# A long convolution shared by two engines: GpSimd's products move to ScalarE, through a ring of six places

## The chip, the cores and the metric

The kernel runs on one core of a Trainium2 chip. The metric is the device time of one execution in microseconds. Five engines work side by side, each through its own queue of instructions in order: TensorE (PE, with its weight loads as PEld), VectorE (DVE), ScalarE (ACT), GpSimd (POOL) and SyncE (SP), which issues most transfers. An instruction waits for others by semaphores; what stands behind it in the queue waits with it.

## The reference

Two blocks follow each other on 512 rows of width 1024. Only the first holds the change: a gated long convolution beside a linear recurrence. The second (attention, then a mixture of 32 experts) takes the larger part of the time and is the same in both kernels.

```python
def first_block(x, c, ...):
    shift, scale, gate = split(silu(c) @ mod_w + mod_b, 3)
    h = rmsnorm(x, norm_g) * (1 + scale) + shift
    cv, cg, cs, lx, ls = split(h @ w_in)          # five times 1024 columns
    v = cv * sigmoid(cg)
    v = causal_depthwise_conv(v, dw_w, dw_b)      # 31 taps per channel
    v = silu(layernorm(v, cln_g, cln_b))
    y_conv = (v @ pw2_w + pw2_b) * silu(cs)
    xs = causal_depthwise_conv(lx, sc_w, sc_b)    # 4 taps
    r = sigmoid(xs @ wr + br); i = sigmoid(xs @ wi + bi)      # per head
    log_a = -8 * r * softplus(-lam)
    hs = linear_scan(exp(log_a), sqrt(-expm1(2 * log_a)) * i * xs)
    y = concatenate([y_conv, hs * silu(ls)]) @ w_out
    return rmsnorm(x + (1 + gate) * y, final_g)   # into second_block
```

A tap of the long convolution multiplies a shifted row of v by one number per channel and adds it to a sum.

## The kernel before

Channels lie on the 128 partitions, the 512 rows along the free dimension; 1024 channels are eight blocks c = 0 to 7. Matrix products are made in three passes from weights and activations split in two parts: `W` (a list of weight loads) casts a piece of 128x2048 to its high part on ScalarE (`whi`, L126) and makes the low part on VectorE (`wlo`, L127).

Eight **conv steps** come first. Step c multiplies h by two pieces of 128 columns (48 matmuls into the PSUM tiles `pcv` and `pcg`), casts the next weights, takes the sigmoid of `pcg` on ScalarE (`sg`, L570) and multiplies on VectorE into `v` (L574). Then `conv31(c)` sets up the 31 taps of that block. The last tap, with the bias, is a scaled activation on ScalarE (`start`, L528). The other 30 are shared out:

- blocks 0, 2 and 4, and two taps of block 7, on GpSimd (`pool_tap`): a product into one scratch place (L537), then a sum into `acc` (L539). These instructions are written into GpSimd's queue at once.
- blocks 1, 3, 5, 6 and the rest of 7 on VectorE: one instruction a tap (`tap`, L532), with the sum in PSUM. They stand in a list, `bg`; `drain(n)` takes n entries from it at fixed places of the code (`DR_0` = 3, `DR_V` = 8, `DR_LX` = 2, `DR_G` = 1, `DR_S` = 6). `join` adds what GpSimd made of block 7 (L543).

Four **recurrence steps** follow, each with two blocks: `lru_in` (product `plx`, its copy L594, the short convolution of three multiply-adds on VectorE L598, the split into two parts L197 and L198), a `silu_proj` of the convolution's outer gate, and `lru_gates` (two small products, two sigmoids L621 and L622). Then `silu_proj(ylru_, 0)` takes what is left in `bg`. GpSimd also keeps a running sum `csum` of some finished blocks (`add_up`, L517 and L519); `means` (L690) needs it and all of `acc`. After that come variances, normalisation and the rest.

The code is written in the order in which the engines run it; no scheduler moves it. `ylru` (eight places) is written by `silu_proj(ylru_, i)` only from the end of the recurrence steps on.

Of the kernel before, what the change touches and what calls it, by code (L numbers as in the profile page):

```python
# [9 lines left out]
F32 = mybir.dt.float32  # L10
# [3 lines left out]
AF = mybir.ActivationFunctionType  # L14
OP = mybir.AluOpType
# [4 lines left out]
S = 512  # L20
# [5 lines left out]
LN_EPS = 1e-5  # L26
ALPHA = 2.0 ** 0.25
LRU_C = 8.0
POOL_CONV = (0, 2, 4)
POOL_TAPS = {7: 2}  # L30
PY = 8
POOL_LN = (0, 1)
BIG = 1024.0
# [121 lines left out]
def block_kernel(ctx, tc, A, out, dbg=None, upto=99):  # L155
    nc = tc.nc
    pe, dve, act, pool, sp = nc.tensor, nc.vector, nc.scalar, nc.gpsimd, nc.sync
    dbg = dbg or {}

    def dump(name, ap):  # L160
        if name in dbg:
            sp.dma_start(out=dbg[name], in_=ap)
# [8 lines left out]
    def psa(name="pa", shape=(128, 512)):  # L171
        return ps.tile(list(shape), F32, tag="a", name=name, bufs=4)

    def pss(name="pss"):
        return ps.tile([128, 2, 512], F32, tag="s", name=name, bufs=2)
# [7 lines left out]
    def mm3(o, l, r, first, last):  # L183

        (lh, ll), (rh, rl) = l, r
        pe.matmul(o, lh, rh, start=first, stop=False)
        pe.matmul(o, lh, rl, start=False, stop=False)
        pe.matmul(o, ll, rh, start=False, stop=last)
# [23 lines left out]
    def k8(t, n=256):  # L212
        return t[:, :8 * n].rearrange("p (k n) -> p k n", k=8)
# [106 lines left out]
    for k in range(8):  # L320
        t = px.tile([128, 2048], F32, tag="mraw", name="mraw", bufs=6)
        for c in range(0, 2048, 2048 if k < 7 else 512):
            n = 2048 if k < 7 else 512
# [39 lines left out]
    def columns(i):  # L363
        pt = psa("ptr")
        pe.transpose(pt[:, 0:128], R3 if i == 3 else R[:, i, :], ident)
        act.copy(out=C[:, i, :], in_=pt[:, 0:128])
# [16 lines left out]
    def dw_col(j, c):  # L383
        n = 8 * j + c
        return C[:, 1 + n // 128, n % 128:n % 128 + 1]
# [31 lines left out]
    for hf in range(2):  # L417
# [4 lines left out]
        for a in range(2):  # L422
            dst = (sB, sA)[hf][:, 4 * a:4 * a + 4]
            dve.tensor_reduce(out=dst, in_=pm[:, a, :].rearrange("p (m n) -> p m n", m=4), axis=mybir.AxisListType.X,
                              op=OP.add)
# [46 lines left out]
    bg = []  # L472

    def drain(n):

        turn = 0
        while n and bg:
            ch_ = bg[turn % min(2, len(bg))]
            ch_.pop(0)()
            if not ch_:  # L480
                bg.remove(ch_)
            turn, n = turn + 1, n - 1

    def proj(o, w, m, xs, nk, n):
        (wh, wl) = w
        wv = [t[:, :nk * n].rearrange("p (k n) -> p k n", k=nk) for t in (wh, wl)]
        for k in range(nk):
            mm3(o, [t[:, k, 128 * m:128 * m + 128] for t in wv], [t[:, k, :] for t in xs], k == 0, k == nk - 1)

    acc = pY.tile([128, 8, NK], F32, tag="acc", name="acc")[:, :, 0:S]  # L490
    scs = [pA.tile([128, 4, S], F32, tag=t, name=t) for t in ("scsh", "scsl")]
    r8 = pA.tile([128, 8, S], F32, tag="r8", name="r8")
    ylru = pY.tile([128, 8, NK], F32, tag="ylru", name="ylru")[:, :, 0:S]

    spare = [pA.tile([128, 4 * S], F32R, tag=t, name=t) for t in ("spareh", "sparel")]
# [9 lines left out]
    def vv(name):  # L505
        return pA.tile([128, S + 32], F32, tag="vv", name=name, bufs=VV)
# [6 lines left out]
    def add_up(c):  # L513

        summed.append(c)
        if len(summed) == 2:
            pool.tensor_tensor(out=csum, in0=acc[:, summed[0], :], in1=acc[:, c, :], op=OP.add)  # L517
        elif len(summed) > 2:
            pool.tensor_tensor(out=csum, in0=csum, in1=acc[:, c, :], op=OP.add)  # L519

    def conv31(c):

        v, st_ = vt[c], {}
        np_ = 30 if c in POOL_CONV else POOL_TAPS.get(c, 0)

        def start():
            st_["o"] = acc[:, c, :] if np_ == 30 else pss("pc")[:, 0, :]
            act.activation(out=st_["o"], in_=v[:, 30:30 + S], func=AF.Identity, scale=dw_col(30, c),  # L528
                           bias=dw_b[:, c:c + 1])

        def tap(j):
            dve.scalar_tensor_tensor(out=acc[:, c, :] if j == 29 and not np_ else st_["o"], in0=v[:, j:j + S],  # L532
                                     scalar=dw_col(j, c), in1=st_["o"], op0=OP.mult, op1=OP.add)

        def pool_tap(j):
            pr_ = spare[1][:, 2 * S:3 * S].bitcast(F32) if j or np_ == 30 else acc[:, c, :]
            pool.tensor_scalar(out=pr_, in0=v[:, j:j + S], scalar1=dw_col(j, c), scalar2=0.0, op0=OP.mult, op1=OP.add)  # L537
            if j or np_ == 30:
                pool.tensor_tensor(out=acc[:, c, :], in0=acc[:, c, :], in1=pr_, op=OP.add)  # L539

        def join():
            if np_:
                dve.tensor_tensor(out=acc[:, c, :], in0=acc[:, c, :], in1=st_["o"], op=OP.add)  # L543
            if c in (1, 3):
                add_up(c)

        if np_ == 30:
            start()
        for j in range(np_):
            pool_tap(j)  # L550
        if np_ == 30:
            add_up(c)
        else:
            bg.append([start] + [(lambda j=j: tap(j)) for j in range(np_, 30)] + [join])

    for c in range(8):
        w = W.get(0)
        if c == 1:
            lru_rates()
        if c == 4:  # L560
            columns(3)
        pcv, pcg = psa("pcv"), psa("pcg")
        wv = [k8(t) for t in w]
        for k in range(8):
            for m, o_ in ((0, pcv), (1, pcg)):
                mm3(o_, [t[:, k, 128 * m:128 * m + 128] for t in wv], [t[:, k, :] for t in (hh, hl)], k == 0, k == 7)
        sg = pA.tile([128, S], F32, tag="sg", name="sg", bufs=2)
        drain(DR_0)
        W.ahead(1)
        act.activation(out=sg, in_=pcg, func=AF.Sigmoid)  # L570
        drain(DR_V)
        v = vt[c] = vv("v")
        dve.memset(v[:, 0:30], 0.0)
        dve.tensor_tensor(out=v[:, 30:30 + S], in0=pcv, in1=sg, op=OP.mult)  # L574
        conv31(c)
    for c in range(8):
        dump(f"v{c}", vt[c][:, 30:30 + S])

# [3 lines left out]
    def lru_in(p):  # L582
        wx = W.get(0)
        for m in range(2):
            c = 2 * p + m
            plx = psa("plx")
            proj(plx, wx, m, (hh, hl), 8, 256)
            lx = lxb[:, m, 0:S + 3]
            dve.memset(lx[:, 0:3], 0.0)
            xs = spare[1][:, S * (c % 2):S * (c % 2 + 1)].bitcast(F32)  # L590
            if m == 0:
                drain(DR_0)
                W.ahead(1)
            act.copy(out=lx[:, 3:], in_=plx)  # L594
            act.activation(out=xs, in_=plx, func=AF.Identity, scale=sc_w[:, 24 + c:25 + c], bias=sc_b[:, c:c + 1])
            drain(DR_LX)
            for j in range(3):
                dve.scalar_tensor_tensor(out=xs, in0=lx[:, j:j + S], scalar=sc_w[:, 8 * j + c:8 * j + c + 1], in1=xs,  # L598
                                         op0=OP.mult, op1=OP.add)
            xs_[c] = xs  # L600
            xsp[c] = [spare[0][:, S * (2 * (c % 2) + n):S * (2 * (c % 2) + n + 1)] for n in range(2)]
            split_to(*xsp[c], xs)
# [11 lines left out]
    def lru_gates(p):  # L614
        wri = gw.pop(0)
        for c in (2 * p, 2 * p + 1):
            pr, pi = psa("pr"), psa("pi")
            mm3(pr, [t[:, 128 * (c % 2):128 * (c % 2) + 128] for t in wri], xsp[c], True, True)
            mm3(pi, [t[:, 256 + 128 * (c % 2):384 + 128 * (c % 2)] for t in wri], xsp[c], True, True)
            ix = ixs[c] = vv("ixs")[:, 0:S]  # L620
            act.activation(out=r8[:, c, :], in_=pr, func=AF.Sigmoid, bias=br[:, c:c + 1])  # L621
            act.activation(out=ix, in_=pi, func=AF.Sigmoid, bias=bi[:, c:c + 1])  # L622
            drain(DR_G)
            dve.tensor_tensor(out=ix, in0=ix, in1=xs_[c], op=OP.mult)

    t2 = {}
# [36 lines left out]
    def silu_proj(dst, i, mid=None, beside=None):  # L663
        w = W.get(1)
        for m in range(2):
            if m and beside:
                beside()
            c = 2 * i + m
            p_ = psa("pcs")
            proj(p_, w, m, (hh, hl), 8, 256)  # L670
            act.activation(out=dst(c), in_=p_, func=AF.Silu)
            drain(DR_S)
            if mid:
                mid(m)

# [40 lines left out]
        (pool if c % 2 else dve).tensor_tensor(out=acc[:, c, :], in0=acc[:, c, :], in1=rsd, op=OP.mult)  # L716
        act.activation(out=acc[:, c, :], in_=acc[:, c, :], func=AF.Silu, scale=ncg[:, c:c + 1], bias=cln_b[:, c:c + 1])

    silu_proj(ylru_, 0, lambda m: drain(1000))
    silu_proj(ylru_, 1, beside=means)  # L720
    silu_proj(ylru_, 2, beside=variances)
    silu_proj(ylru_, 3, lambda m: [normal(c) for c in range(8) if m == 0])
# [16 lines left out]
    for i in range(4):  # L739
# [12 lines left out]
        for m in range(2):  # L752
            c = 2 * i + m
            dve.scalar_tensor_tensor(out=yc[:, c, :], in0=pps[m], scalar=pw2_b[:, c:c + 1], in1=scs_(c),
                                     op0=OP.add, op1=OP.mult)
# [684 lines left out]
    for hf in range(2):  # L1440
# [3 lines left out]
        for i in range(4):  # L1444
# [12 lines left out]
            for g, p_ in ((1, pb), (0, pa)):  # L1457
                dve.scalar_tensor_tensor(out=hr[:, i, sl_], in0=p_, scalar=rst[:, i, g:g + 1], in1=hr[:, i, sl_],
                                         op0=OP.mult, op1=OP.add)
# [29 lines left out]
    for i in range(4):  # L1489
# [3 lines left out]
                             op0=OP.mult, op1=OP.add)  # L1493
# [513 lines left out]
    for p in range(NE):  # L2007
        before, midst = beside(p)
        for j, e, g, q_ in passes(p):
            if p == NE - 1 and j == 13:  # L2010
# [4 lines left out]
                for i in range(4):  # L2015
                    dve.tensor_scalar(out=oT[:, i, :], in0=iotab, scalar1=its[NI - 1]["tk"][:, i:i + 1], scalar2=None,
                                      op0=OP.is_equal)
# [30 lines left out]
            elif p > 1:  # L2048
# [7 lines left out]
                             op0=OP.mult, op1=OP.subtract)  # L2056
    sums_, late_ = [], []
    for i in range(4):
        if i < 2:
            o = [psa("po") for c in range(2)]  # L2060
        else:
            t = pss("po")
            o = [t[:, c, :] for c in range(2)]
# [61 lines left out]
```

## Time and profile before

| | us |
|---|---|
| median of 3 runs | 1946.8 (1946.47 to 1949.99) |
| the profiled execution | 1946.13 |
| its span | 1944.0 |

Over the span TensorE is busy 91%, VectorE 60%, ScalarE 40%, GpSimd 26%. These are averages over parts with different limits. The long convolution lies between about 54 and 305 us of the span, and GpSimd is nearly full there, as the second part of the page shows (each column is a slice of 48.6 us):

```profile
PE   4899777979997999899998899999979999999995
DVE  6799975866656556797531437166334556868613
ACT  5224533633345443472420425145223444646401
POOL 3899995531211211410100000101100110010102
```

Each digit is the busy share of a slice in tenths. In the third to sixth slice GpSimd stands at 9; ScalarE is there between 2 and 5.

### The profile page before, as it was taken

Reading aid. Unit: us, or ns where it says so; the run is one execution under the profiler, and the core shown is the slowest. Engines: PE = TensorE matmul, PEld = TensorE weight load, DVE = VectorE, ACT = ScalarE, POOL = GpSimd, SP = SyncE. Lnnn points to the kernel's source line nnn. Section 1 sums busy time; section 2 is a strip of 40 time slices with the busy share of each in tenths; the row PEclk is TensorE's granted clock in tenths of the full one; section 3 lists DMA queues with packets and bytes.
Section 4 is the critical chain, followed back from the end, with each engine's and each line's share of the span. In section 5 each row is a group of like instructions: output and inputs, shape, how many; then the busy total and the mean of one; then the engine's idle time right before and its main releaser. Section 6 shows DMA issues by size and latency. Waiting matters only on the chain. (4 is left out here: it accounts for less than half of the span.)

```text
span 1944.0 us, 21937 instructions
## 1 busy us (share of the span) xinstructions
PE 1764.0 (91%) x8001; PEld 1135.3 (58%) x8001; DVE 1171.5 (60%) x1548; ACT 781.8 (40%) x930; POOL 514.7 (26%) x402
## 2 busy tenths in 40 slices
PE   4899777979997999899998899999979999999995
PEld 3687665758886777675542446365435555767621
DVE  6799975866656556797531437166334556868613
ACT  5224533633345443472420425145223444646401
POOL 3899995531211211410100000101100110010102
PEclk8999898989998999899999999999999999999998
DMA  8322221263221007699999979999996999999994
GB/s 292 87 71 70 76 87 65 87 234 114 88 70 44 1 1 276 244 313 348 396 401 400 372 241 405 397 406 399 400 395 219 395 403 401 407 380 406 375 406 188
DMA packets 174126, 503.48 MB, mean 259 GB/s; under 512 B 15691, under 2 KB 57809, under 8 KB 172992
## 3 DMA queue, kind: packets, MB, share of 16 engines
q1 hardware_dynamic: 162032, 475.22, 64.5%
q0 software_dynamic: 11248, 25.45, 4.6%
q8 instruction: 64, 1.05, 0.2%
q10 hardware_dynamic: 736, 1.38, 0.2%
q14 instruction: 46, 0.38, 0.1%
HBM read 489.45 MB, written 20.76 MB: 262 GB/s over the span
## 5 line engine op out<-in xcount | busy, mean ns | idle before, releaser
L127 DVE TENSOR_TENSOR wlo<-wraw,whi 128x2048 fp32r<-128x2048 f32 (+1 forms) x213 | 485.8, 2291 | 188.6 <-ACT whi L126 187.6
L126 ACT CAST whi<-wraw 128x2048 fp32r<-128x2048 f32 (+1 forms) x213 | 402.2, 1890 | 164.1 <-PE pg L1870 71.5
L1851 PE MATMUL pg<-wraw,xTs 128*64 128x512 f32 x1280 | 306.8, 607 | 11.0 <-DMA wraw<-w_gate_up 10.6
L1608 POOL DMA_INDIRECT acc_d<-y,ix x33 | 52.4, 1587 | 869.0 <-ACT y L1834 386.8
L1851 PE MATMUL pg<-wraw,ats 128*64 128x512 f32 x640 | 157.1, 615 | 23.6 <-ACT ats L1816 14.8
L1851 PEld LDWEIGHTS pg<-wraw,xTs 128*64 128x64 f32 x1280 | 80.9, 137 | 165.8 <-issue 133.0
L1870 PE MATMUL pg<-whi,xTh 128*128 128x512 f32 x448 | 149.3, 415 | 0.0
L1870 PE MATMUL pg<-wlo,xTh 128*128 128x512 f32 x448 | 141.2, 397 | 0.0
L1870 PE MATMUL pg<-whi,xTl 128*128 128x512 f32 x448 | 140.1, 394 | 0.0
L1601 DVE TENSOR_SCALAR lp<-pg 128x256 f32<-128x256 f32 (+1 forms) x68 | 36.1, 530 | 158.0 <-ACT sg L1600 158.0
L539 POOL TENSOR_TENSOR acc<-acc,sparel 128x512 f32<-128x512 f32 x91 | 129.1, 1419 | 7.7 <-ACT acc L528 0.2
L532 DVE SCALAR_TENSOR_TENSOR pc<-v,C,pc 128x512 f32<-128x512 f32 x144 | 101.6, 747 | 2.1 <-ACT pc L528 0.8
L537 POOL TENSOR_SCALAR sparel<-v,C 128x512 f32<-128x512 f32 x91 | 97.9, 1076 | 15.1 <-DVE V L454 6.4
L1851 PEld LDWEIGHTS pg<-wraw,ats 128*64 128x64 f32 x640 | 41.7, 139 | 101.8 <-issue 72.5
L1870 PEld LDWEIGHTS pg<-whi,xTh 128*128 128x128 f32 x448 | 78.3, 190 | 38.0 <-issue 23.9
L1870 PEld LDWEIGHTS pg<-whi,xTl 128*128 128x128 f32 x448 | 85.1, 190 | 19.6
L1870 PEld LDWEIGHTS pg<-wlo,xTh 128*128 128x128 f32 x448 | 84.7, 190 | 19.9 <-DVE wlo L127 0.7
L1816 ACT COPY ats<-pat 128x256 f32<-128x256 f32 x40 | 14.9, 372 | 193.8 <-PE pat L1614 193.8
L1544 POOL DMA_INDIRECT xg<-h_d,ix x34 | 61.6, 1813 | 82.8 <-issue 40.5
L1525 DVE COPY pi<-pidx 128x5 f32<-128x5 f32 (+2 forms) x36 | 5.8, 162 | 123.3 <-PE pidx L1523 123.3
L1600 ACT ACTIVATE sg<-pg 128x256 f32<-128x256 f32 (+1 forms) x68 | 32.2, 474 | 115.4 <-PE pg L1851 56.6
L1870 PE MATMUL pg<-whi,ath 128*128 128x512 f32 x224 | 73.6, 410 | 0.0
(663 smaller groups left out, 3387.0 us busy)
## 6 DMA issues: line engine op xcount, KB each, us to landing
wraw<-w_gate_up SPq DMA_DIRECT2D x256, 1024.0 KB, 17.9
wraw<-w_down SPq DMA_DIRECT2D x128, 1024.0 KB, 18.8
wraw<-w_in SPq DMA_DIRECT2D x17, 1024.0 KB, 5.2
wraw<-w_out SPq DMA_DIRECT2D x8, 1024.0 KB, 4.8
mraw<-mod_w SPq DMA_DIRECT2D x7, 1024.0 KB, 13.5
wraw<-w_in SPq DMA_DIRECT2D x14, 512.0 KB, 4.7
wraw<-pw_w SPq DMA_DIRECT2D x4, 1024.0 KB, 5.1
wraw<-mod_w SPq DMA_DIRECT2D x4, 1024.0 KB, 5.0
```

The costliest lines, as they stand in the source:

```text
L126: self.nc.scalar.copy(out=hi[:, c], in_=t[:, c])
L127: self.nc.vector.tensor_tensor(out=lo[:, c], in0=t[:, c], in1=hi[:, c].bitcast(F32), op=OP.subtract)
L532: dve.scalar_tensor_tensor(out=acc[:, c, :] if j == 29 and not np_ else st_["o"], in0=v[:, j:j + S], scalar=dw_col(j, c), in1=st_["o"], op ...
L537: pool.tensor_scalar(out=pr_, in0=v[:, j:j + S], scalar1=dw_col(j, c), scalar2=0.0, op0=OP.mult, op1=OP.add)
L539: pool.tensor_tensor(out=acc[:, c, :], in0=acc[:, c, :], in1=pr_, op=OP.add)
L1544: pool.indirect_dma_start(out=xg, out_offset=None, in_=src, in_offset=bass.IndirectOffsetOnAxis(ap=ix, axis=0), bounds_check=n - 1, oob_is ...
L1600: act.activation(out=sg, in_=v2[:, :, :, 0], func=AF.Sigmoid, scale=1.702)
L1601: dve.tensor_scalar(out=lp, in0=v2[:, :, :, 1], scalar1=-6.0, scalar2=8.0, op0=OP.max, op1=OP.min)
L1608: pool.indirect_dma_start(out=dst, out_offset=bass.IndirectOffsetOnAxis(ap=ix, axis=0), in_=y, in_offset=None, bounds_check=n - 1, oob_is_ ...
L1816: act.copy(out=it["at"][:, c:c + 2, :], in_=it["pa"].pop(c))
L1851: pe.matmul(it["acc"][g][64 * c:64 * c + 64, 0, :], it["parts"][g, 2 * q_ + k], wv[:, k, 512 * c:512 * c + 512], start=False, stop=q_ == 3 ...
L1870: pe.matmul(it["acc"][g][:, c, :], l, r[:, k, 512 * c:512 * c + 512], start=False, stop=end)
```

## The change

Blocks 0, 2, 4 and 6 now lie on GpSimd, 1, 3, 5 and 7 on VectorE, each whole. GpSimd makes no products. ScalarE makes them (an activation with a scale per partition) into six places of `ylru` (2 to 7) in turn, and GpSimd adds each to `acc`. Product and sum of a tap are written together, from a list `ag`, by `pooled(n)`, at fixed places: 4 before the sigmoid of a conv step, 7 after its `conv31`, 3 at six places of a recurrence step. A product that reuses a place waits for the sum that read it, six products earlier.

```diff
-POOL_CONV = (0, 2, 4)
-POOL_TAPS = {7: 2}
+POOL_CONV = (0, 2, 4, 6)
+AD_0, AD_V, AD_L = 4, 7, 3
...
+    ag, prods = [], [0]
+
+    def pooled(n):
+
+        for _ in range(min(n, len(ag))):
+            ag.pop(0)()
...
         def pool_tap(j):
-            pr_ = spare[1][:, 2 * S:3 * S].bitcast(F32) if j or np_ == 30 else acc[:, c, :]
-            pool.tensor_scalar(out=pr_, in0=v[:, j:j + S], scalar1=dw_col(j, c), scalar2=0.0, op0=OP.mult, op1=OP.add)
-            if j or np_ == 30:
-                pool.tensor_tensor(out=acc[:, c, :], in0=acc[:, c, :], in1=pr_, op=OP.add)
-
-        def join():
-            if np_:
-                dve.tensor_tensor(out=acc[:, c, :], in0=acc[:, c, :], in1=st_["o"], op=OP.add)
-            if c in (1, 3):
+            pr_ = ylru[:, 2 + prods[0] % 6, :]
+            prods[0] += 1
+            act.activation(out=pr_, in_=v[:, j:j + S], func=AF.Copy, scale=dw_col(j, c))
+            pool.tensor_tensor(out=acc[:, c, :], in0=acc[:, c, :], in1=pr_, op=OP.add)
+            if j == 29:
                 add_up(c)
 
-        if np_ == 30:
+        if own:
             start()
-        for j in range(np_):
-            pool_tap(j)
-        if np_ == 30:
-            add_up(c)
+            ag.extend([(lambda j=j: pool_tap(j)) for j in range(30)])
         else:
-            bg.append([start] + [(lambda j=j: tap(j)) for j in range(np_, 30)] + [join])
+            bg.append([start] + [(lambda j=j: tap(j)) for j in range(30)]
+                      + ([lambda: add_up(c)] if c in (1, 3) else []))
...
         drain(DR_0)
         W.ahead(1)
+        pooled(AD_0)
         act.activation(out=sg, in_=pcg, func=AF.Sigmoid)
...
         conv31(c)
+        pooled(AD_V)
...
             drain(DR_LX)
+            pooled(AD_L)
...
             drain(DR_G)
+            pooled(AD_L)
...
             drain(DR_S)
+            pooled(AD_L)
...
-    silu_proj(ylru_, 0, lambda m: drain(1000))
+    silu_proj(ylru_, 0, lambda m: [pooled(1000), drain(1000)])
```

The first place is ScalarE's queue at conv steps 6 and 7 (`sg` the sigmoid, `whi` the cast of weights, `pc` the start of a chain on VectorE), before:

```order
L570 ACTIVATE sg<-pcg 128x512 [waits PE_49,Activation_49]
L528 ACTIVATE pc<-v,C 128x512 [waits DVE_49]
L126 CAST whi<-wraw 128x2048 [waits DMAHW2_49,DMAHW1_49,Activation_49]
L570 ACTIVATE sg<-pcg 128x512 [waits PE_49,Activation_49]
L126 CAST whi<-wraw 128x2048 [waits DMAHW3_49,Activation_49]
L570 ACTIVATE sg<-pcg 128x512 [waits PE_49,Activation_49]
```

The same place in the changed kernel (`ylru<-v,C` is a product into the ring, `acc<-v,C` the start of block 6):

```order
L572 ACTIVATE sg<-pcg 128x512 [waits PE_49]
L535 ACTIVATE acc<-v,C 128x512 [waits DVE_49]
L545 ACTIVATE ylru<-v,C 128x512 [waits Pool_49] x7
L126 CAST whi<-wraw 128x2048 [waits DMAHW3_49]
L545 ACTIVATE ylru<-v,C 128x512 [waits Pool_49] x4
L572 ACTIVATE sg<-pcg 128x512 [waits PE_49]
L545 ACTIVATE ylru<-v,C 128x512 [waits Pool_49] x7
```

Eleven products now stand between one sigmoid and the next, and each waits for GpSimd (`Pool`); before, nothing on ScalarE waited for it here.

The second place is VectorE's queue in recurrence step 3 (`pc<-v,C,pc` is a tap, `sparel` the short convolution, `gw` the gates' weights), before:

```order
L589 MEMSET lx 128x3
L532 SCALAR_TENSOR_TENSOR pc<-v,C,pc 128x512 x2
L598 SCALAR_TENSOR_TENSOR sparel<-lx,C,sparel 128x512 [waits DVE_49,Activation_49]
L598 SCALAR_TENSOR_TENSOR sparel<-lx,C,sparel 128x512 [waits DVE_49] x2
L198 TENSOR_TENSOR spareh<-sparel,spareh 128x512 [waits PE_49,Activation_49]
L532 SCALAR_TENSOR_TENSOR pc<-v,C,pc 128x512 x2
L532 SCALAR_TENSOR_TENSOR pc<-v,C,pc 128x512 [waits DVE_49] x2
L532 SCALAR_TENSOR_TENSOR acc<-v,C,pc 128x512 [waits DVE_49]
L532 SCALAR_TENSOR_TENSOR pc<-v,C,pc 128x512 [waits DVE_49]
L198 TENSOR_TENSOR gw<-wraw,gw 128x512 [waits DMAHW1_49,DMAHW2_49,PE_49,Activation_49]
L127 TENSOR_TENSOR wlo<-wraw,whi 128x2048 [waits DMAHW3_49,PE_49,Activation_49]
L532 SCALAR_TENSOR_TENSOR pc<-v,C,pc 128x512 [waits DVE_49] x6
```

The same place in the changed kernel:

```order
L592 MEMSET lx 128x3
L602 SCALAR_TENSOR_TENSOR sparel<-lx,C,sparel 128x512 [waits DVE_49,Activation_49]
L602 SCALAR_TENSOR_TENSOR sparel<-lx,C,sparel 128x512 [waits DVE_49] x2
L198 TENSOR_TENSOR spareh<-sparel,spareh 128x512 [waits PE_49,Activation_49]
L198 TENSOR_TENSOR gw<-wraw,gw 128x512 [waits DMAHW1_49,DMAHW2_49,PE_49,Activation_49]
L127 TENSOR_TENSOR wlo<-wraw,whi 128x2048 [waits DMAHW3_49,PE_49,Activation_49]
```

The taps are gone from this step: VectorE's list is empty by the end of recurrence step 2. On GpSimd the alternation of L537 and L539 becomes an unbroken row of sums, each of which waits for ScalarE and for the sum before it.

## Rows read from the trace of the kernel before

**Rows 1.** Timeline of ScalarE: start us, us, engine, line, operation, tiles [idle before].

```profile
84.52 0.60 ACT L570 ACTIVATE sg<-pcg 128x512 f32<-128x512 f32 x1 [10.12 <-PE pcg L188]
85.88 0.82 ACT L528 ACTIVATE acc<-v,C 128x512 f32<-128x512 f32 x1 [0.76 <-DVE v L574]
...
140.61 0.60 ACT L570 ACTIVATE sg<-pcg 128x512 f32<-128x512 f32 x1 [8.76 <-PE pcg L188]
141.10 1.90 ACT L126 CAST whi<-wraw 128x2048 fp32r<-128x2048 f32 x1
...
335.15 5.76 ACT L717 ACTIVATE acc<-acc,C,V 128x512 f32<-128x512 f32 x8 [0.27 <-DVE acc L716]
```

**Rows 2.** Page, part 5: line, engine, operation, count | busy us, mean ns | idle before.

```profile
L532 DVE SCALAR_TENSOR_TENSOR pc<-v,C,pc 128x512 f32<-128x512 f32 x144 | 101.6, 747 | 2.1 <-ACT pc L528 0.8
L537 POOL TENSOR_SCALAR sparel<-v,C 128x512 f32<-128x512 f32 x91 | 97.9, 1076 | 15.1 <-DVE V L454 6.4
```

**Rows 3.** One line, GpSimd's sums: count, duration ns min/median/max, first and last start.

```profile
L539 POOL TENSOR_TENSOR acc<-acc,sparel x91: 1260/1296/3332, 55.9 to 302.2; 128x512 f32<-128x512 f32 x91
```

**Rows 4.** Waits, 45 to 345 us: who waited for whom, us, times, longest.

```profile
PE pmu L690 <- POOL sparel L519: 17.4, 1, 17.4
```

**Rows 5.** Busy time by stretch: length, engines' busy us (instructions), PEclk, DMA, GB/s.

```profile
84.52:140.61 56.09, 56.09 (x243) 45.21 (x242) 51.28 (x65) 15.43 (x16) 52.27 (x43) 1.00 0.27 80
141.10:206.89 65.79, 57.11 (x230) 44.96 (x229) 62.76 (x73) 30.12 (x37) 61.53 (x48) 0.95 0.23 72
206.89:271.38 64.49, 52.91 (x206) 41.38 (x205) 61.28 (x67) 28.53 (x35) 60.51 (x46) 0.89 0.24 78
271.38:287.40 16.02, 15.93 (x69) 12.59 (x67) 11.38 (x14) 6.25 (x6) 14.93 (x13) 1.00 0.32 101
287.40:304.70 17.30, 0.00 (x0) 0.00 (x0) 1.23 (x2) 0.54 (x1) 16.11 (x17) 0.61 0.00 0
66.00:71.20 5.20, 0.00 (x0) 0.00 (x0) 5.06 (x10) 0.00 (x0) 4.92 (x4) 0.82 0.00 0
71.20:75.00 3.80, 3.80 (x9) 3.02 (x10) 2.64 (x4) 2.60 (x2) 3.52 (x4) 0.50 0.70 196
```

The engines stand in the order PE, PEld, DVE, ACT, POOL.

**Rows 6.** Timeline of GpSimd, columns as in rows 1.

```profile
68.95 3.33 POOL L539 TENSOR_TENSOR acc<-acc,sparel 128x512 f32<-128x512 f32 x1
...
93.72 0.69 POOL L537 TENSOR_SCALAR sparel<-v,C 128x512 f32<-128x512 f32 x1
94.50 1.28 POOL L539 TENSOR_TENSOR acc<-acc,sparel 128x512 f32<-128x512 f32 x1
95.88 0.69 POOL L537 TENSOR_SCALAR sparel<-v,C 128x512 f32<-128x512 f32 x1
...
149.35 1.01 POOL L537 TENSOR_SCALAR sparel<-v,C 128x512 f32<-128x512 f32 x1
...
217.50 1.63 POOL L517 TENSOR_TENSOR sparel<-acc 128x512 f32<-128x512 f32 x1
...
298.16 2.60 POOL L519 TENSOR_TENSOR sparel<-sparel,acc 128x512 f32<-128x512 f32 x2
```

**Rows 7.** Timeline of VectorE: rates of the recurrence, then a low half.

```profile
64.81 1.13 DVE L464 TENSOR_SCALAR V<-V 128x8 f32<-128x8 f32 x1
...
68.33 0.56 DVE L468 TENSOR_SCALAR V<-V 128x8 f32<-128x8 f32 x1
...
68.87 2.28 DVE L127 TENSOR_TENSOR wlo<-wraw,whi 128x2048 fp32r<-128x2048 f32 x1
```

**Rows 8.** Groups by line and shape, columns as in rows 2.

```profile
L598 DVE SCALAR_TENSOR_TENSOR sparel<-lx,C,sparel 128x512 f32<-128x512 f32 x24 | 31.3, 1303 | 0.6
L654 DVE SCALAR_TENSOR_TENSOR gacc<-wraw,V,gacc 128x1024 f32<-128x1024 f32 x2 | 2.6, 1284 | 6.1 <-DMA wraw<-mod_w 6.1
L690 PE MATMUL pmu<-acc,ones 128*128 128x512 f32 x6 | 3.6, 744 | 0.0
L690 PE MATMUL pmu<-sparel,ones 128*128 128x512 f32 x2 | 2.1, 1141 | 17.4 <-POOL sparel L519 17.4
```

More of the change, by code (lines that the diff above doesn't have):

```diff
@@ L519, in add_up @@
             pool.tensor_tensor(out=csum, in0=csum, in1=acc[:, c, :], op=OP.add)
+    ag, prods = [], [0]
+    def pooled(n):
+        for _ in range(min(n, len(ag))):
+            ag.pop(0)()
     def conv31(c):
         v, st_ = vt[c], {}
-        np_ = 30 if c in POOL_CONV else POOL_TAPS.get(c, 0)
+        own = c in POOL_CONV
         def start():
-            st_["o"] = acc[:, c, :] if np_ == 30 else pss("pc")[:, 0, :]
+            st_["o"] = acc[:, c, :] if own else pss("pc")[:, 0, :]
             act.activation(out=st_["o"], in_=v[:, 30:30 + S], func=AF.Identity, scale=dw_col(30, c),
@@ L531, in tap @@
         def tap(j):
-            dve.scalar_tensor_tensor(out=acc[:, c, :] if j == 29 and not np_ else st_["o"], in0=v[:, j:j + S],
+            dve.scalar_tensor_tensor(out=acc[:, c, :] if j == 29 else st_["o"], in0=v[:, j:j + S],
                                      scalar=dw_col(j, c), in1=st_["o"], op0=OP.mult, op1=OP.add)
         def pool_tap(j):
-            pr_ = spare[1][:, 2 * S:3 * S].bitcast(F32) if j or np_ == 30 else acc[:, c, :]
-            pool.tensor_scalar(out=pr_, in0=v[:, j:j + S], scalar1=dw_col(j, c), scalar2=0.0, op0=OP.mult, op1=OP.add)
-            if j or np_ == 30:
-                pool.tensor_tensor(out=acc[:, c, :], in0=acc[:, c, :], in1=pr_, op=OP.add)
-        def join():
-            if np_:
-                dve.tensor_tensor(out=acc[:, c, :], in0=acc[:, c, :], in1=st_["o"], op=OP.add)
-            if c in (1, 3):
+            pr_ = ylru[:, 2 + prods[0] % 6, :]
[3 more added lines that the diff above has]
+            if j == 29:
                 add_up(c)
-        if np_ == 30:
+        if own:
             start()
-        for j in range(np_):
-            pool_tap(j)
-        if np_ == 30:
-            add_up(c)
-        else:
-            bg.append([start] + [(lambda j=j: tap(j)) for j in range(np_, 30)] + [join])
+            ag.extend([(lambda j=j: pool_tap(j)) for j in range(30)])
+        else:
+            bg.append([start] + [(lambda j=j: tap(j)) for j in range(30)]
+                      + ([lambda: add_up(c)] if c in (1, 3) else []))
     for c in range(8):
```

## The prediction

> **What bounds the kernel now.** I read the page first, for which engines work in the convolution, then the waits of 45 to 345 us, then the stretch cut by ScalarE's own landmarks (its sigmoids and weight casts [rows 1]), and last single instructions on GpSimd.
>
> The long convolution is 31 taps on eight blocks of channels. One tap on GpSimd is two instructions, a product (L537) and a sum (L539): 91 of each; a product takes 1.08 us in the mean, a sum 1.30 us in the median, each with the disturbances that it meets [rows 2, 3]. One tap on VectorE is one instruction of 0.75 us [rows 2]. The end of the convolution is a wait: TensorE stands idle 17.4 us for GpSimd's running sum before the means [rows 4], and from 287.4 to 304.7 us TensorE does nothing, VectorE 1.2 us, GpSimd 16.1 of 17.3 us [rows 5]. So at its end the stretch hangs on GpSimd. Before that it does not. Between the sigmoids of the conv steps 2 and 7 TensorE is busy 56.1 of 56.1 us, 11.2 us a step [rows 5]. In the two recurrence steps after 141.1 us VectorE is the fullest, 62.8 of 65.8 us, and again in the last two, 61.3 of 64.5 us. Today nothing there waits for GpSimd: it runs its pairs of instructions on its own and is waited for once.
>
> **What the change does to that.** GpSimd's work falls from 91 products and 91 sums to 120 sums. But ScalarE's products stand in ScalarE's queue between the casts and sigmoids that feed TensorE and VectorE, and a product may start only when the sum six places before it has been made. GpSimd thus gets many waiters where it had one. A sigmoid has behind it VectorE's multiply into v, the free PSUM banks that TensorE needs, and the next cast of weights. I number the products: 7 in conv step 0, 11 in each later one, 18 in each of the recurrence steps 0 and 1. At the sigmoid of conv step 7, 77 are issued, so sum 71 is made.
>
> **The pace of GpSimd.** A sum takes 1.28 us and the next instruction starts 0.10 later: 94.50 to 95.88 us is 1.38 us [rows 6]. Two dependent sums in a row took 2.60 us, 1.30 each, which is the lower end. When VectorE makes the low half of a weight (wlo, L127, 2.28 us at 68.87 us [rows 7]) the sum beside it takes 3.33 us: 2.0 us are lost, once per conv step. So a conv step that waits for GpSimd lasts 11 x 1.38 + 2.0 = 17.2 us, against 11.2 us.
>
> Here a rule of the Trainium skill can be weighed, and it speaks against the change. The rows have GpSimd's one-input product at 0.69 us undisturbed and the two-input sum at 1.30 us [rows 3, 6]. GPSIMD Engine Reference, section 4.1 (Engine selection), says the same in kind: additions of two tensors are about half as fast as on VectorE, operations with one input run near line rate; so the change leaves GpSimd the slower half. From the 4497 ns that the page (section 3.1) gives for 2048 elements, 512 would be 1.12 us, an estimate; with the gap of the rows 92 sums would take 15 us less than below, and the time would be 1953. The row decides.
>
> **The sum, stage by stage** (the times before are the instants of [rows 1] and the stretches of [rows 5], cut at ScalarE's weight casts).
>
> 1. Start to the sigmoid of conv step 2 (84.52 us): seven products stand before the Exp of the recurrence's rates, 7 x 0.72 = 5.0 us (0.72 is the pace of eight scaled activations, 5.76 us; the start instruction of a tap chain with 0.82 us bounds it). The tiny VectorE instructions of the rates wait for whatever GpSimd has running, 0.56 us behind a product and 1.13 behind a sum [rows 7]; with sums alone the five short ones become long: 2.9 us. Together +7.9. Both hang before TensorE's next weights, which come from the same VectorE queue; it idled there already, 66 to 71.2 us [rows 5]. Bounds: +2.9, if the products run where VectorE waits anyway, and 7 x 0.82 + 2.9 = +8.6.
>
> 2. Sigmoid 2 to sigmoid 7, before 56.1 us. The first product comes 2.9 us after the sigmoid (1.36 to the start, 0.82, 0.72). Then sums 23 to 71 must pass: 49 x 1.38 = 67.6, five wlo at 2.0 = 10.0, two adds of the running sum 2.7, one product 0.7. That is 83.9 us: +27.8. TensorE's 11.2 us and VectorE's 10.3 us of a step fit in 17.2.
>
> 3. Sigmoid 7 to the weight cast behind it, before 0.5 us: seven products need sums 72 to 78, 9.7 us: +9.2.
>
> 4. Recurrence steps 0 and 1, before 65.8 us: 36 sums are 49.7 us. What VectorE takes from GpSimd there: from 149.35 to 217.50 us 24 taps took 68.15 us [rows 6], undisturbed (93.72 to 95.88 us) 24 x 2.16 = 51.8, so 16.3 are lost; three adds 4.0. Together 70.0 us. Upper bound: the 18 products of a step are 13.0 us on ScalarE, which idles 17.8 us of a step (35.7 in both); if half of them fall where it did not idle, 78.8 us. I take 72, near the first, since the idle time is longer than the products: +6.2.
>
> 5. Recurrence steps 2 and 3, before 64.5 us, now without GpSimd's work and with 24 entries fewer in VectorE's queue (18 left in step 2, none in step 3): about 23 taps, 16 us. The three multiply-adds of the short convolution fall too, from 1.30 us beside GpSimd to about 0.66 (1.28 us for twice the width with GpSimd idle [rows 8]): 12 x 0.64 = 7.7. VectorE falls to some 38 us, and TensorE is next with 52.9 busy. I take 55: -9.5; bounds -11.6 (TensorE without a gap) and -5.8 (half of its gaps of 11.6 us stay).
>
> 6. From there to the means, before 33.3 us, of which TensorE works 15.9 [rows 5]: the wait goes, -17.3. GpSimd's last sum is then some 60 us old.
>
> 7. The means: TensorE no longer comes from 17 us of idling (1.14 us for its first product against 0.74 later [rows 8]) and has three blocks to add instead of four: -2.
>
> Sum: 7.9 + 27.8 + 9.2 + 6.2 - 9.5 - 17.3 - 2 = +22.3 us. All later work is the same and shifts. The profiled execution took 1946.1 us, 0.7 under the median of the three runs, 1946.8. Forecast 1946.1 + 22.3 = 1968 us. Its own range: 92 sums at 1.30 instead of 1.38 us are -7; the other lower bounds are -5 in stage 1, -2 in 4 and -2 in 5, the upper ones +0.7, +6.8 and +3.7: 1952 to 1979.
>
> **Rivals.**
>
> The ring holds nobody (faster). If GpSimd keeps up, stages 1 to 4 stay as they are and 5, 6 and 7 give 28.8 us: 1917. For it: GpSimd loses 91 products, 98 us, and gets 29 sums, 38 us; its last sum comes earlier in any case. The place is the ring in the conv steps, and the pace decides: to fit 11.2 us a sum may take (11.2 - 2.0) / 11 = 0.84 us; the gain is gone at 1.38 - 22.3/92 = 1.14 us. Against: the shortest of 91 sums took 1.26 us [rows 3]. Chance 8 in 100.
>
> The loss falls on VectorE. If a chain of sums without gaps keeps VectorE's two-input instructions waiting instead of being held up, stage 2 loses the 10 us of wlo and stage 4 half of its 16: +4.3, 1950 us. Against: the sum beside wlo took 3.33 us, wlo itself no more than 2.28. SBUF — State Buffer, section "Who interferes with whom", says that whichever instruction is first keeps the shared port to its end, so that the order decides who is held. The rows show both: wlo holding a sum, and sums holding the rates. Chance 7 in 100.
>
> TensorE becomes the bound. It would idle 6 us in each conv step of 17.2. After the 5.2 us of idling before 71.2 us the granted clock was 0.50, which is 1.2 GHz, for the next 3.8 us [rows 5]: about 2 us a step, inside the 6 us. If the lower clock lasted the whole step, it would take 22.4 us, and five of them +26: 1994. Bubbles on ScalarE in stage 4 beyond its bound belong here too, since they come from the same queue. Chance 11 in 100.
>
> **Chances and range.** Forecast 74, the rivals 8, 7 and 11. The range from 1950 to 1984 holds the forecast, most of the second rival and the near part of the third. A measurement of this kernel can tell 0.2%, 3.9 us. Faster by more: 8, and 1 of the second rival; within: 4 of the second rival and 1 of the forecast; slower: 86.
>
> **What will show it.** Sums on GpSimd at 1.38 us in a row during the conv steps, with no idle time, and sigmoids 17 us apart instead of 11; ScalarE's longest waits on the products, for GpSimd's sums; TensorE idle some 6 us in each conv step; the cast before the recurrence at about 186 us; no wait of TensorE for GpSimd before the means, which start near 327 us. I am wrong if the sigmoids stay 11 us apart, or if GpSimd idles in the conv steps (then the products, not the sums, set the pace), or if the means come before 305 us.

## The result and the profile after

| | us |
|---|---|
| the kernel before, median of 5 runs | 1948.1 (1946.47 to 1949.99) |
| the changed kernel, median of 5 runs | 1968.2 (1964.07 to 1970.08) |
| ratio | 1.010, 95% interval 1.0086 to 1.0113 |
| profiled execution of the changed kernel | 1964.07, span 1961.8 |

The change made the kernel slower by 1%. The forecast was 1968, of the side "slower". Between the two profiled executions the difference is 17.9 us, between the medians 20.1; the forecast added 22.3 us to a profiled execution of 1946.1, which lies 2.0 under the median of the five runs. That 1968 meets the median of 1968.2 so closely is in part luck: the two errors of 2 us cancel.

Much of the prediction's mechanism can be seen on ScalarE alone. This is its timeline in the changed kernel, around the sigmoid of conv step 3 and from the sigmoid of step 7 to the cast before the recurrence (start, us, engine, line, tiles, idle before):

```profile
91.72 0.60 ACT L572 ACTIVATE sg<-pcg 128x512 f32<-128x512 f32 x1 [8.09 <-PE pcg L188]
...
99.89 1.95 ACT L545 ACTIVATE ylru<-v,C 128x512 f32<-128x512 f32 x3
103.49 0.72 ACT L545 ACTIVATE ylru<-v,C 128x512 f32<-128x512 f32 x1 [1.65 <-POOL acc L546]
104.12 0.58 ACT L572 ACTIVATE sg<-pcg 128x512 f32<-128x512 f32 x1
...
174.26 0.58 ACT L572 ACTIVATE sg<-pcg 128x512 f32<-128x512 f32 x1
175.00 0.73 ACT L545 ACTIVATE ylru<-v,C 128x512 f32<-128x512 f32 x1 [0.16 <-POOL acc L546]
176.37 0.73 ACT L545 ACTIVATE ylru<-v,C 128x512 f32<-128x512 f32 x1 [0.64 <-POOL acc L546]
...
183.83 1.88 ACT L126 CAST whi<-wraw 128x2048 fp32r<-128x2048 f32 x1
```

At 104 us the sigmoid starts at once when the fourth product is out: it no longer waits for TensorE, as in [rows 1], but for the product in front of it, and that waits for GpSimd. From 175 us the products start 1.37 us apart, half of it waiting: that is GpSimd's rhythm on ScalarE's queue. Sigmoid 2 to sigmoid 7 take 82.5 us, 16.5 a step, against 11.2 before.

GpSimd's sums in that stretch, by the view of one line (duration min/median/max), and who waited for whom between 45 and 345 us (us, times, longest):

```profile
L546 POOL TENSOR_TENSOR acc<-acc,ylru x50: 1261/1294/3308, 94.6 to 173.7; 128x512 f32<-128x512 f32 x50
```

```profile
ACT ylru L545 <- POOL acc L546: 28.9, 33, 2.3
POOL acc L546 <- ACT ylru L545: 16.9, 5, 6.9
...
PE pcv L188 <- DVE v L575: 14.0, 1, 14.0
...
ACT sg L572 <- PE pcg L188: 11.6, 2, 8.1
```

Fifty sums start from 94.6 to 173.7 us, 1.61 us each with the two adds of the running sum and five low halves of weights between them; the longest, beside such a half, took 3.31. The wait of the sigmoids for TensorE was, in the kernel before and by the same view:

```profile
ACT sg L570 <- PE pcg L188: 51.7, 8, 10.1
```

It shrank from eight times to two, both before 92 us (3.5 and 8.1 us), so none of the sigmoids of steps 3 to 7 waited for TensorE; in its place ScalarE waited 33 times for GpSimd. TensorE's wait for GpSimd before the means [rows 4] is gone, and its longest idle time, 14.0 us, lies at the start, beside the recurrence's rates. Those rates on VectorE:

```profile
74.53 1.12 DVE L468 TENSOR_SCALAR V<-V 128x8 f32<-128x8 f32 x1
75.56 0.16 DVE L469 TENSOR_SCALAR V<-V 128x8 f32<-128x8 f32 x1
75.64 2.28 DVE L127 TENSOR_TENSOR wlo<-wraw,whi 128x2048 fp32r<-128x2048 f32 x1
```

L468 took 0.56 us before [rows 7], behind a product; now it stands behind a sum. The busy times by stretch, cut at the same landmarks as in [rows 5] (columns as there):

```profile
91.72:174.26 82.54, 66.61 (x256) 51.02 (x255) 49.53 (x63) 51.99 (x71) 75.93 (x52) 0.90 0.18 55
183.83:255.34 71.51, 52.52 (x191) 39.78 (x192) 65.35 (x66) 50.29 (x73) 64.22 (x40) 0.83 0.21 66
255.34:309.12 53.78, 49.06 (x202) 38.83 (x201) 39.94 (x48) 28.27 (x36) 9.48 (x6) 0.94 0.32 103
309.12:325.00 15.88, 15.88 (x69) 12.76 (x68) 5.36 (x4) 6.53 (x7) 0.00 (x0) 1.00 0.20 68
```

In the first stretch GpSimd is the fullest engine, 75.9 of 82.5 us, and 5.4 of the rest is its one wait at the start. In the third, nearly without GpSimd (9.5 us), VectorE fell from 61.3 to 39.9 us, TensorE is the fullest, and the stretch is 10.7 us shorter than before. In the fourth TensorE works without a gap up to the means:

```profile
324.40 1.02 PE L696 MATMUL pmu<-sparel,ones 128*128 128x512 f32 x2
```

### The profile page after: what moved, and what is told of

Same layout as the page of the kernel before. It is cut to its first block, busy times and chain, and to the rows that moved or that the text cites. A ratio compares the mean times of both kernels' runs of the same rounds, so it can differ in the third digit from the quotient of the medians.

```text
span 1961.8 us, 22058 instructions
## 1 busy us (share of the span) xinstructions
PE 1766.3 (90%) x7999; PEld 1135.3 (58%) x7999; DVE 1149.8 (59%) x1519; ACT 857.1 (44%) x1050; POOL 471.4 (24%) x340
## 3 DMA queue, kind: packets, MB, share of 16 engines
q10 hardware_dynamic: 736, 1.38, 0.2%
## 5 line engine op out<-in xcount | busy, mean ns | idle before, releaser
L546 POOL TENSOR_TENSOR acc<-acc,ylru 128x512 f32<-128x512 f32 x120 | 182.0, 1517 | 25.7 <-ACT ylru L545 16.9
L545 ACT ACTIVATE ylru<-v,C 128x512 f32<-128x512 f32 x120 | 80.0, 717 | 29.1 <-POOL acc L546 28.9
L539 DVE SCALAR_TENSOR_TENSOR pc<-v,C,pc 128x512 f32<-128x512 f32 x116 | 82.5, 749 | 2.1 <-ACT pc L535 0.8
```

The source lines that it names most:

```text
L539: dve.scalar_tensor_tensor(out=acc[:, c, :] if j == 29 else st_["o"], in0=v[:, j:j + S], scalar=dw_col(j, c), in1=st_["o"], op0=OP.mult, o ...
L545: act.activation(out=pr_, in_=v[:, j:j + S], func=AF.Copy, scale=dw_col(j, c))
```

## The experiments

Theories: (A) ScalarE is held by the ring at GpSimd's pace, and its queue holds all others; (B) 120 products are too much work for ScalarE; (C) GpSimd's sums slow VectorE by themselves, or TensorE's lower clock does it. Ratios are to the kernel before; the instants are from the profiles.

**e1: a deeper ring.** Eight more places in tiles that are written only later.

```diff
-            pr_ = ylru[:, 2 + prods[0] % 6, :]
+            places = [ylru[:, k, :] for k in range(2, 8)] + [scs_(k) for k in range(4, 8)] + [r8[:, k, :] for k in range(4, 8)]
+            pr_ = places[prods[0] % 14]
```

> The changed kernel with a ring of 14 places instead of six (eight more in tiles that are written only from recurrence step 2 on). Theory (ScalarE is held by the ring, at GpSimd's 1.37 us a sum): a product waits for the sum 14 before it, so the sigmoid of conv step 7 comes 8 sums, about 11 us, earlier than in the changed kernel (174 us), and about as much is left at the end: 1955 to 1960. Rival (the 120 products are too much work for ScalarE): depth does not matter, 1966 to 1970. Rival (VectorE and TensorE slowed by the shared port or the clock): no change either.

Measured 1957.1 us, ratio 1.0054 (1.0037 to 1.0072). The sigmoid of step 7:

```profile
163.32 0.58 ACT L573 ACTIVATE sg<-pcg 128x512 f32<-128x512 f32 x1
```

10.9 us earlier than with six places: eight sums. The same products, sums and VectorE work, only more room. Neither B nor C changes with the depth of a ring; A does. Not all of it lasts: at the start of the means 7.3 us are left in the profile, since GpSimd's row ends hardly earlier (263.7 us, 265.2 in the changed kernel) and so reaches further into recurrence steps 2 and 3. VectorE's short convolution, held by the sums there, takes 14.5 us instead of 10.9, and the two steps 57.6 instead of 53.8.

**e2: the same products, spread.**

```diff
-AD_0, AD_V, AD_L = 4, 7, 3
+AD_0, AD_V, AD_L = 3, 4, 3
```

> The changed kernel with 3, 4 and 3 products at its places instead of 4, 7 and 3: 7 a conv step and 18 in each of the four recurrence steps, the same 120 in all. Theory: seven sums and one low half of a weight are 7 x 1.37 + 2.0 = 11.6 us a step, and TensorE needs 11.2, so the ring holds ScalarE little before the recurrence; stages: +4 to the sigmoid of step 2, +1 to step 7, +3 behind it, +6 in recurrence steps 0 and 1, +2 in steps 2 and 3 (no longer free of GpSimd), -17 for the wait before the means, -2.5 in the means: 4 us faster than before, 1938 to 1946. Rival (too much work for ScalarE): the same 120 products cost the same 20 us, 1965 or more.

Measured 1945.7 us, ratio 0.9996 (0.9987 to 1.0005): no change against the kernel before, and by the ratios 20 us less than the changed kernel. B falls as the main cause: ScalarE made all 120 products. The gain that was expected over the kernel before did not come; its stretches:

```profile
87.66:147.33 59.67, 57.19 (x243) 44.94 (x241) 46.77 (x58) 37.75 (x52) 50.20 (x33) 1.00 0.24 71
151.45:225.38 73.93, 57.19 (x225) 43.87 (x224) 69.64 (x76) 50.52 (x72) 63.64 (x40) 0.91 0.20 64
225.38:291.56 66.18, 53.09 (x202) 40.51 (x201) 54.13 (x48) 46.45 (x66) 58.94 (x36) 0.87 0.25 79
```

The conv steps lost 3.6 us, not 1; recurrence steps 0 and 1 lost 8.1, not 6; steps 2 and 3 lost 1.7, as expected. With 3.1 us up to sigmoid 2 and 3.6 behind sigmoid 7, about as expected, that pays back the 17 us of the wait.

**e3: half sums.** GpSimd adds 256 of 512 columns; ScalarE's products are whole. This leaves out half of each sum.

```diff
-            pool.tensor_tensor(out=acc[:, c, :], in0=acc[:, c, :], in1=pr_, op=OP.add)
+            pool.tensor_tensor(out=acc[:, c, 0:256], in0=acc[:, c, 0:256], in1=pr_[:, 0:256], op=OP.add)
```

> The changed kernel with GpSimd's sums over the first 256 of 512 columns only; ScalarE's products stay whole. Leaves out half of each sum. Theory: a sum takes about 0.75 us, 11 and a low half 10.2 us a conv step, under TensorE's 11.2; the ring holds nobody, stages 2 and 3 fall from +35 to about +7 (the products themselves behind the last sigmoid, 5 us), and the time is below before: 1930 to 1942. Rival (too much work for ScalarE, 11 x 0.64 us and a cast, a sigmoid and a start a step): unchanged, 1964 to 1970.

Measured 1998.9 us, ratio 1.0287 (1.0263 to 1.0310). As a time the expectation missed, since other numbers come out of the first block: the experts chosen from them differ, and a loop for overfull experts that ran no round in the changed kernel ran here. The transfers of that loop, by the view of DMA issues (count, KB each, us to landing):

```profile
wl<-w_gate_up SPq DMA_DIRECT2D x8, 1024.0 KB, 8.0
wl<-w_down SPq DMA_DIRECT2D x4, 1024.0 KB, 4.8
```

So this run is read up to the means only:

```profile
281.35 1.02 PE L696 MATMUL pmu<-sparel,ones 128*128 128x512 f32 x2
```

That is 43 us before the changed kernel and 23 before the kernel before: with sums of 0.74 us GpSimd held ScalarE for 0.8 us in all. But the stretch from sigmoid 2 to sigmoid 7 still took 64.7 us, 8.6 more than before, and the last products added 4.3:

```profile
83.16:147.90 64.74, 59.62 (x243) 46.74 (x241) 46.34 (x58) 49.83 (x72) 48.27 (x54) 0.95 0.22 65
```

ScalarE is not full here, 49.8 of 64.7 us; it also waits 11.3 us for VectorE's v. Once the ring holds nobody, a conv step is a chain through both queues, v, eleven products and a cast, the next sigmoid, at 13 us in the mean. So a weaker form of B is the second bound: not the number of products, but their place between v and the next sigmoid, some 13 of the 35 us of stages 2 and 3.

**e4: no products.** GpSimd's 120 sums read v; ScalarE makes none. This leaves out the products.

```diff
-            act.activation(out=pr_, in_=v[:, j:j + S], func=AF.Copy, scale=dw_col(j, c))
-            pool.tensor_tensor(out=acc[:, c, :], in0=acc[:, c, :], in1=pr_, op=OP.add)
+            pool.tensor_tensor(out=acc[:, c, :], in0=acc[:, c, :], in1=v[:, j:j + S], op=OP.add)
```

> The changed kernel without ScalarE's products: GpSimd's 120 sums read v instead of the ring. Leaves out the products. Theory: GpSimd runs its 120 sums unheld and holds nobody; they end at about 55 + 120 x 1.37 + 20 low halves x 2.0 + 17 for the rest = 277 us, before the means at about 285; stages 1 to 4 near before, the wait of 17 us gone: 1922 to 1932. Rival (the sums on GpSimd slow VectorE by the shared port, whoever waits): 1950 or more. Rival (TensorE's clock): follows the idle time, so as the theory.

Measured 2168.0 us, ratio 1.1147 (1.1127 to 1.1168), by three rounds of the same loop (24 and 12 transfers), so again only the way to the means counts: they start at 287.23 us, 37 before the changed kernel. Sigmoid 2 to sigmoid 7, and recurrence steps 0 and 1:

```profile
87.10:143.18 56.08, 56.08 (x243) 45.19 (x242) 50.55 (x65) 16.24 (x16) 53.43 (x37) 1.00 0.27 80
143.68:209.87 66.19, 54.99 (x220) 42.99 (x219) 63.17 (x67) 29.28 (x36) 63.29 (x42) 0.92 0.22 70
```

They take 56.1 and 66.2 us, as before, with GpSimd as busy as before. Full sums on GpSimd that hold nobody cost nothing there, so the first half of C falls as the main cause. The second half, the clock, this run can't test, since TensorE does not idle between the sigmoids in it; against it stands that in the changed kernel no sigmoid from step 3 to step 7 waited for TensorE. GpSimd was through with them at 250.6 us, not 277: what VectorE would take from it was counted too high.

**e5: the rates first.** The rates of the recurrence in conv step 0, ahead of GpSimd's first sum.

```diff
-        if c == 1:
+        if c == 0:
             lru_rates()
```

> The changed kernel with the recurrence's rates made in conv step 0, ahead of GpSimd's first sum, instead of step 1. Theory (GpSimd's row of sums is the path from sum 1 to the last product): VectorE's rates get short and TensorE's idling of 14 us goes, but of that only what kept GpSimd waiting (5.4 us before its sum 23), less some 1.5 us later start, is left at the sigmoid of conv step 7: 170 us instead of 174, and 1962 to 1966. Rival (TensorE's path through the weights is the bound, so that its 14 us of idling count): sigmoid 7 at 165 or earlier, 1955 to 1960.

Measured 1960.5 us, ratio 1.0073 (1.0057 to 1.0088). TensorE's wait of 14.0 us became 1.3, but the sigmoid of step 7 came only 4.1 us earlier, at

```profile
170.20 0.58 ACT L572 ACTIVATE sg<-pcg 128x512 f32<-128x512 f32 x1
```

where the theory had put it: what is gained ahead of GpSimd's row is waited for behind it. The profiled execution gained 3.1 us; by the ratios it is some 5. As a time the expectation missed by a little: 1960.5 lies between its 1962 and the 1960 of the rival, so the instant decides, not the time.

**e6 and e8: the same edit elsewhere.** e6 has it beside 3, 4, 3; e8 is the kernel before with this edit alone.

> The 3, 4, 3 distribution with the rates in conv step 0. Theory: here TensorE paces the conv steps, so its idling of 10.3 us beside the rates counts in full, less 2 us for the later first sum and 1 us of sums that now come closer together: 7 us faster than the 3, 4, 3 kernel, 1936 to 1942, faster than both kernels. Rival (GpSimd's row is the path here too): at most 2 us, 1943 or more.

> The kernel before with the rates in conv step 0 and nothing else. Theory: its conv hangs on GpSimd, whose 91 products and sums are not held by the rates; TensorE's 6.0 us of idling go and come back as a longer wait before the means; GpSimd starts up to 2 us later: 1946 to 1949, no change. Rival (TensorE's 6 us count): 1940 to 1942.

e6: 1939.7 us, ratio 0.9959 (0.9946 to 0.9973). e8: 1946.7 us, ratio 0.9998 (0.9986 to 1.0009). By the ratios one edit is worth 0 in the kernel before, some 5 us in the changed one and some 7 in the spread one; each of these is known to 3 or 4 us, so the last two are not told apart, but neither is 0. In e8 the sigmoid of step 7 came 7.7 us earlier, and all of it went into the wait at the end, 17.4 us before [rows 4], now:

```profile
PE pmu L690 <- POOL sparel L519: 26.1, 1, 26.1
```

**e7: products where ScalarE waits.** As e6, but a recurrence step's 18 products stand 6 and 6 behind the start of the short convolution and 3 and 3 behind the gates' sigmoids.

```diff
-AD_0, AD_V, AD_L = 3, 4, 3
+AD_0, AD_V, AD_L, AD_G, AD_S = 3, 4, 6, 3, 0
...
             drain(DR_G)
-            pooled(AD_L)
+            pooled(AD_G)
...
             drain(DR_S)
-            pooled(AD_L)
+            pooled(AD_S)
```

> As the 3, 4, 3 kernel with early rates, but the 18 products of a recurrence step stand 6 and 6 behind the short convolution's start (where ScalarE waits some 5 us for VectorE) and 3 and 3 behind the gates' sigmoids, none before the cast of the gates' weights. Theory (in the recurrence steps the products cost what they delay in ScalarE's queue, about 2.7 us a step, the gates' weights above all): 4 to 8 us less than without this, 1930 to 1937. Rival (the steps are longer because GpSimd's sums hold VectorE, wherever the products stand): no change within 2 us.

Measured 1930.5 us (1926.97 to 1935.79), ratio 0.9914 (0.9900 to 0.9928): faster than both kernels. Its recurrence steps 0 and 1, then 2 and 3, took 69.2 and 64.3 us, against 74.0 and 66.2 in e6 (its two rows stand first):

```profile
142.73:216.69 73.96, 57.88 (x225) 44.31 (x224) 69.67 (x76) 50.53 (x72) 63.67 (x40) 0.88 0.20 64
216.69:282.89 66.20, 52.98 (x204) 40.82 (x203) 54.13 (x48) 46.45 (x67) 58.96 (x36) 0.90 0.25 79
142.59:211.81 69.22, 55.19 (x218) 43.06 (x217) 66.14 (x74) 51.64 (x72) 66.31 (x41) 0.90 0.22 69
211.81:276.06 64.25, 52.86 (x212) 41.05 (x211) 55.06 (x51) 47.61 (x67) 57.58 (x35) 0.92 0.23 73
```

The work is the same, so the place of the products alone is worth this. VectorE's busy time of the first stretch fell from 69.7 to 66.1 us too, so part of the gain may be in which of its instructions meet a sum. How much is that and how much the queue was not separated.

## Why the prediction was right, step by step

By the profiles, with the landmarks of the prediction:

| stage | predicted | measured |
|---|---|---|
| 1, start to sigmoid 2 | +7.9 | +7.2 |
| 2, sigmoid 2 to 7 | +27.8 | +26.4 |
| 3, to the cast | +9.2 | +9.1 |
| 4, recurrence steps 0 and 1 | +6.2 | +5.7 |
| 5, recurrence steps 2 and 3 | -9.5 | -10.7 |
| 6, to the means | -17.3 | -18.0 |
| 7, the means | -2 | -2.5 |
| sum | +22.3 | +17.2 |

Stage 7 is measured from the first product of the means to the first normalised block, 30.4 us before and 28.0 after. All seven errors lie on one side and add up to 5 us; the shift at the means' end, 17.2 us, is the difference of the profiled executions, 17.9, within a microsecond, so nothing happened later.

Right: the pace of a sum, 1.37 us apart against 1.38; the 2.0 us of a low half, 3.31 us for the sum beside it; sigmoid 7 at 174 us against 176; the cast at 184 against 186; the means at 324 against 327. e1 shows that it is the ring, e2 that it is not the number of products, e4 that unheld sums hold nobody.

One sign came out smaller: TensorE was to idle some 6 us in each conv step, and between sigmoids 2 and 7 it idled 15.9 us, 3.2 a step. Its work there took 66.6 us instead of 56.1, at a granted clock of 0.90 instead of 1.00. By the mean matmul of the stretch before, 0.23 us, some 3 of these 10.5 us are 13 more matmuls (an estimate); the rest, 1.5 us a step, is near the 2 us that the third rival had for the clock.

Too high: stage 1 counts seven products of 0.72 us, and in a row they took 4.39, 0.63 each. Of the rates six instructions grew and not five: five from 0.56 us to 1.12, and L459 from 0.24 to 1.09. Stages 1 and 2 are not two independent terms: e5 takes all of the growth of stage 1 away, 8.5 us at sigmoid 2, but gains 4.1 us at sigmoid 7, because GpSimd's row of sums then waits less at its start and is waited for more. In stage 5 the short convolution fell to 0.91 us in the mean, 0.75 at its shortest, and not to 0.66; the stage still came out shorter than predicted, since TensorE, which is next, had 49.1 us of work and not 52.9.

Stage 4 was taken near GpSimd's own pace, and that is the step that was wrong though its size was right. From 183.8 to 255.3 us ScalarE waited for GpSimd once, 1.1 us; GpSimd waited for ScalarE three times, 4.6 us. What is late is what stands behind a product. The timeline of step 0, around the gates' first product (PE's wait in brackets):

```profile
205.08 1.93 ACT L545 ACTIVATE ylru<-v,C 128x512 f32<-128x512 f32 x3
...
206.92 0.61 ACT L197 CAST gw<-wraw 128x512 fp32r<-128x512 f32 x1
...
207.62 0.76 PE L186 MATMUL pr<-spareh,gw 128*128 128x512 f32 x1 [6.24 <-POOL acc L546]
```

The product needs the gates' weights gw, whose cast came behind three products, 1.9 us; that the wait is put down to a sum of GpSimd, which it does not read, is the profile's guess. In the kernel before the same product waited 0.7 us, its third part 3.3 for the weights' low half. VectorE's short convolution also got slower, by the view of groups in this stage (count, busy us, mean ns, idle before), before and after:

```profile
L598 DVE SCALAR_TENSOR_TENSOR sparel<-lx,C,sparel 128x512 f32<-128x512 f32 x12 | 15.4, 1280 | 0.3
L602 DVE SCALAR_TENSOR_TENSOR sparel<-lx,C,sparel 128x512 f32<-128x512 f32 x12 | 20.5, 1712 | 0.3
```

In e4 it took 1.59 us beside a GpSimd as busy, and the stage 66.2 us, so the sums alone do not make the 5.7 us: these come with the products in ScalarE's queue. How much of them is the late cast, and how much VectorE's meetings with sums in their new order, the runs did not separate.

The rivals: the ring that holds nobody was priced at 1917, with the means 27 us before those of the kernel before. In e3, whose ring held next to nobody, they came 23 us earlier, and not as the rival has it: stages 2 and 3 were 13 us longer than before, and the recurrence steps 17 us shorter, where the rival has 9.5. The loss that falls on VectorE did not show in the conv steps: sums beside low halves still took 3.3 us, and the five low halves there 2.53 us each in the mean, against 2.75 before. (The prediction read "no more than 2.28" off one low half; in the trace of before these five took 2.28 to 3.28.) In the recurrence steps part of it did show, in the short convolution. The clock fell to 0.90 in the conv steps' stretch, and TensorE had 16 us of its 82.5 to spare.

## What to carry to other kernels

Moving half of an operation to a freer engine joins two queues: in a short ring the producer runs at the consumer's pace, and everything behind the producer in its queue does too. So compare the pace of the slowest member, with what disturbs it, with the pace of the stage, and place the pieces so that each stage gets what the slow engine can do in it: here seven sums a conv step instead of eleven, the same work, turned +20 us into none. The worth of an edit then depends on who is the path at that place; the same move of the rates was worth nothing in one kernel and some 5 to 7 us in two others.

## What was not expected of the hardware

Every second one of VectorE's instructions of 8 elements a partition took 1.09 to 1.24 us beside GpSimd's row of sums. In e5, where the rates run ahead of the first sum, the two that are shown above took:

```profile
51.75 0.17 DVE L468 TENSOR_SCALAR V<-V 128x8 f32<-128x8 f32 x1
51.83 0.17 DVE L469 TENSOR_SCALAR V<-V 128x8 f32<-128x8 f32 x1
```

The prediction had the long ones from [rows 7], but not that they alternate so regularly: in the changed kernel the long ones at L464 start 1.36 us apart, which is the pace of GpSimd's sums. That fits a small instruction that waits out the sum in progress, however small its own work, with the next one slipping in between two sums; the trace does not split the 1.1 us into wait and work. A sum of 256 columns took 0.74 us against 1.29 for 512, so half the width costs a little more than half the time.
